# Ten and five wide expert places instead of eleven and five, the last two narrow, and a weight ring cut later, in a two-layer transformer kernel

## The chip, the cores and the metric

The kernel runs on one core of a Trainium2 chip, as one program. The metric is the device time of one execution in microseconds (us); the number compared is the median over several executions. Before the change it is 1600.03 us (three runs, 1596.84 to 1610.28).

## What is computed

The reference is a two-layer transformer trunk on 256 image tokens and 256 context tokens of width 1024. Each layer has a mixer (a gated linear attention, a Fourier mix and a windowed attention, merged by gates) and then a mixture of 16 experts. Layer 0 sends all 512 tokens through its experts, layer 1 only the 256 image tokens; a final norm follows. The change lies in the experts' part:

```python
def hierarchical_moe(h, w_router_group, w_router_expert, w1, w3, w2):
    ...
    expert_id = g_sel[:, None] * MOE_EXPERTS_PER_GROUP + top_idx
    ...
    for e in range(MOE_EXPERTS):
        hid = jax.nn.silu(h @ w1[e]) * (h @ w3[e])
        out = out + (hid @ w2[e]) * gates[:, e:e + 1]
    return out
```

Every token has two experts. An expert's three matrices (1024x512, 1024x512, 512x1024, float32) are 6 MiB.

## The kernel before

The order of the program is mixer 0, experts 0, mixer 1, experts 1, final norm (`body`). The kernel does not run each expert over all tokens. It sorts the tokens by expert and works through 16 **places** in a fixed order (`moe`); which expert stands at which place is decided on the chip. The first `STAT` places (two in layer 0, three in layer 1) hold experts 0, 1 (and 2); the other experts are ranked by their number of tokens, and the ranks are dealt first to the wide places and then to the narrow ones (`place_ranks`).

- A **wide** place, `B` in `PLACES`, has room for 128 tokens. Each weight piece is split by ScalarE and VectorE into a high and a low part (`split`, lines 265 and 266), and TensorE makes three products per pair of tiles (`mm3`, lines 235 to 237): 72 products of 128x512 in a place.
- A **narrow** place, `s`, has room for 64 tokens. The weights are used as they are, in float32, without splitting. `pair` (line 1643) sets two products side by side in the column halves of TensorE: `w1` and `w3`, and later the two column halves of `w2`. The trace shows 32 + 16 records of line 1643 in a place.

If an expert has more tokens than its place has room, a branch (`tc.If`, line 1768) runs `moe_general`, which goes through all 16 experts again for every 256 tokens.

**Weights and ring.** A place's weights come in six pieces of 1 MiB, 96 in a layer, loaded by DMAs that SyncE's queue issues in the order of `pieces_of` (all have line 245 in the profile). In that order stand, for place q, the second halves of its `w1` and `w3`, the first piece or pieces of place q+1 (one for a wide place, two for a narrow one), and the two `w2` pieces of place q; counted from 1, the `w2` pieces of the last places are 84 and 85 or later. Each piece gets the next slot of a ring (`ring`). In layer 0 the ring has 12 slots: six of its own, two of the pool `raw`, and four **spare** ones; in layer 1 it has 13. A piece's DMA is issued when the piece that last held the slot has been used, and SyncE's queue is in order, so nothing behind it is issued earlier. After `CUT` pieces the spare slots drop out as they come up, and eight (nine) are left. The spare slots are wanted at the end of the stage:

- For the places up to the last but two, outputs are scaled by the gate (`ye`, lines 1719 and 1732) and scattered to a table `yb` in HBM by GpSimd's indirect DMA (line 1561).
- The outputs of the last two places stay on the chip: line 1739 and line 1740 write their high and low parts into spare slots (`yes`).
- `rows` (line 1747) loads the scattered outputs back in token order, two rows for each token, into spare slots, after the last weight piece; GpSimd adds the two (line 1748).
- `put_rows` adds the last two places with products against a one-hot matrix (line 1759) and the loaded rows with a product against the identity (line 1762), into one PSUM tile for each 512 columns; part of it stands before the branch of line 1768 and part behind.
- Then the sum is scaled (line 1780), added to `x` (line 1782), and in layer 1 normed and written out (lines 407, 408, 416, 1847, 1848).

The tile framework schedules each engine's order from the program's order and its dependencies; instructions of neighbouring places interleave. TensorE starts the next place's first products before the current place's `w2` products.

The functions that the change touches and what calls them:

Of the kernel before, what the change touches and what calls it, by code (L numbers as in the profile page):

```python
# [8 lines left out]
F32 = mybir.dt.float32  # L9
F32R = mybir.dt.float32r  # L10
# [3 lines left out]
AF = mybir.ActivationFunctionType  # L14
OP = mybir.AluOpType
# [4 lines left out]
P = 128  # L20
# [4 lines left out]
NE = 16  # L25
CAP = (128, 128)
SM = 64

STAT = (2, 3)
PLACES = ("BBsBBsBBsBBsBsBB", "BBBsssssssssssBB")  # L30
RING = (6, 7)
ONCE = (0, 2)
AHEADG = 2
CUT = 50
EXTRA = 2
EA = 8
EB = 1
# [10 lines left out]
def consts():  # L48
# [47 lines left out]
    for l in range(2):  # L96
        big = np.array([x == "B" for x in PLACES[l]])
        pos[:, l, 0] = NE - 1 - np.arange(NE) + 1.0e5 * np.maximum(0, STAT[l] - np.arange(NE))
# [9 lines left out]
def place_ranks(l):  # L108

    n = STAT[l] + PLACES[l][STAT[l]:].count("B")  # L110
    big, small = iter(range(n)), iter(range(n, NE))
    return [next(big if x == "B" else small) for x in PLACES[l]]


def ts(i, n):
    return slice(i * n, (i + 1) * n)
# [12 lines left out]
class Net:  # L129
# [1126 lines left out]
    def ring(self):  # L1256

        self.piece += 1
        if self.piece > CUT:

# [5 lines left out]
    def pieces_of(self, l):  # L1266
# [9 lines left out]
        def up(w, q, c):  # L1276
            return (w, q, c), self.wload(src(w, q)[ts(c, 512), :], 4, 512, self.ring())
# [5 lines left out]
        def begin(q):  # L1283
            for w in ("w1", "w3")[:1 + (PLACES[l][q] == "s")]:
                yield up(w, q, 0)
        self.eid = {}
        yield from begin(0)
        for q in range(NE):
            yield up("w1", q, 1)
            if PLACES[l][q] == "B":  # L1290
                yield up("w3", q, 0)
# [109 lines left out]
    def moe(self, l):  # L1401
        nc, io, tc = self.nc, self.io, self.tc
        T = 2 * SEQ if l == 0 else SEQ
        nt = T // P
        ns, cap = T // SEQ, CAP[l]
        big = [x == "B" for x in PLACES[l]]
        dp, h2b, yb, lg = self.dp, self.h2b, self.yb, self.lg
# [3 lines left out]
        def tl(shape, name, dt=F32):  # L1411
            return dp.tile(shape, dt, name=name)
        V = nc.vector
# [46 lines left out]
        for c in range(2):  # L1460
            pt = self.c1()
            for k in range(4):
                for t in range(nt):
                    nc.tensor.matmul(pt[:, ts(k, cap)], self.h2[:, t, ts(4 * c + k, P)], self.oh0[:, t],
                                     start=(t == 0), stop=(t == nt - 1))
# [45 lines left out]
        yp = self.pool(sr, "moey", bufs=3, side="right")  # L1511
# [3 lines left out]
        gsl = tl([P, NE], "gsl")  # L1515
# [116 lines left out]
        def up(ps, xx, w, e, c):  # L1632

            for u, (wh, wl) in enumerate(self.halves(w, e, c)):
                for k in range(2):
                    kk = 4 * c + 2 * u + k
                    self.mm3(ps, xx[0][:, kk, :], xx[1][:, kk, :], wh[:, k, :], wl[:, k, :], kk == 0, kk == KD - 1)

        def pair(ps, xs, ws, k0, n):

            for k in range(n):
                for i, w in enumerate(ws):
                    nc.tensor.matmul(ps[ts(i, SM)], xs[:, k0[0] + k, :], w[:, k, :], start=(k0[0] + k == 0),  # L1643
                                     stop=(k0[0] + k == k0[1] - 1))

        def begin(e, xx):
            ps = self.pA()
            if big[e]:
                up(ps, xx, "w1", e, 0)
            else:  # L1650
                pair(ps, xx, [self.piece_at(w, e, 0) for w in ("w1", "w3")], (0, KD), 4)
            return ps
# [6 lines left out]
        def hidden(th, n):  # L1659
            pt = self.c3()  # L1660
            for k in range(4):
                nc.tensor.transpose(pt[:, ts(k, n)], th[:, ts(k, P)], self.ident[:n, :n])
            return pt[:, :4 * n]
        yes = []
        p1 = begin(0, xx)
        for e in range(NE):
            if big[e]:
# [6 lines left out]
            if big[e]:  # L1674
# [5 lines left out]
                pt = hidden(th, cap)  # L1680
# [3 lines left out]
            else:  # L1684
# [4 lines left out]
                pt = hidden(th, SM)  # L1689
# [11 lines left out]
            if e == NE - 2:  # L1701
# [4 lines left out]
                oh = rp.tile([P, 2, T], F32R, name="oh")  # L1706
                for i in range(2):
                    for t in range(nt):
                        V.tensor_scalar(oh[:cap, i, ts(t, P)], self.iotab[:cap], float(P * t - 1), tkf[:cap, e + i:e + i + 1],
                                        op0=OP.add, op1=OP.is_equal)  # L1710
                rq = self.pool(sr, "rows2", bufs=2, side="right") if nt > 2 else None
            if not big[e]:
                p2 = self.c2()
                for c in range(2):
                    w = self.piece_at("w2", e, c)
                    for k in range(2):
                        pair(p2, hs, [w[:, k:k + 1, ts(o, 512)] for o in range(2)], (2 * c + k, 4), 1)
                ye = yp.tile([P, 512], F32, name="ye")
                nc.scalar.activation(ye, p2, AF.Copy, scale=gsl[:, e:e + 1])  # L1719
                put = (ye, e)  # L1720
                continue
            p2 = [self.c2(), self.c2()]
            for c in range(2):
# [5 lines left out]
            if e < NE - 2:  # L1729
                ye = yp.tile([P, D], F32, name="ye")  # L1730
                for o in range(2):
                    nc.scalar.activation(ye[:, ts(o, 512)], p2[o], AF.Copy, scale=gsl[:, e:e + 1])
                put = (ye, e)
                continue
            ye = self.spare.pop(0).tile([P, 2048], F32, name="wraw").bitcast(F32R).rearrange("p (h d) -> p h d", h=2)
            yes.append(ye)
            for o in range(2):
                q = ts(o, 512)
                nc.scalar.activation(ye[:cap, 0, q], p2[o][:cap], AF.Copy, scale=gsl[:cap, e:e + 1])
# [1 line left out]
                                       op0=OP.mult, op1=OP.subtract)  # L1741
# [11 lines left out]

        def put_rows(t, pt, js):

            for o in range(2):
                for j in js:
                    for u in range(2):
                        nc.tensor.matmul(pt[o], oh[:cap, j, ts(t, P)], yes[j][:cap, u, ts(o, 512)],  # L1759
                                         start=(j + u == 0), stop=False)  # L1760
                if 1 in js:
                    i = nc.tensor.matmul(pt[o], self.ident, yrs[t][:, 0, ts(o, 512)], start=False, stop=True)  # L1762
                    self.lates += [i] if t >= 2 else []
        pts = [[self.pA(), self.pA()], [self.c1(), self.c1()]]
        for t in range(2):
            put_rows(t, pts[t], (0,))
# [4 lines left out]
        for t in range(nt):  # L1771
            self.pri.append(tc.cur_priority)
            yr = yrs[t]
            if t < 2:
                pt = pts[t]
                put_rows(t, pt, (1,))
            else:
                pt = [self.c1(), self.c2()]
                put_rows(t, pt, (0, 1))
            i = [V.tensor_mul(yr[:, 1, ts(o, 512)], pt[o], gb[:, t // 2, ts(o, 512)]) for o in range(2)]  # L1780
            self.later += i if t >= 2 else []
            V.tensor_add(self.x[:, t], self.x[:, t], yr[:, 1])
# [116 lines left out]
```

## Time and profile before

| | us |
|---|---|
| median of three runs | 1600.03 |
| lowest, highest | 1596.84, 1610.28 |
| the profiled execution, device time | 1606.12 |
| its span, first to last instruction | 1604.30 |
| PE (TensorE) busy | 1465.3 |
| VectorE busy | 972.2 |
| ScalarE busy | 765.4 |

PE is TensorE's products, PEld its weight loads, DVE is VectorE, ACT ScalarE, POOL GpSimd, SP SyncE. Times in the rows count from the span's start. A wait is shown as idle time in front of an instruction, with what ended it. Places are counted from 0 to 15.

### The profile page before, as it was taken

To read this page: it belongs to the slowest core of one execution; us is meant where nothing else is said; L and a number is where in the kernel's file an instruction comes from. 1 tells how busy PE (TensorE), PEld (TensorE's weight loads), DVE (VectorE), ACT (ScalarE), POOL (GpSimd) and SP (SyncE) were. 2 spreads that over 40 slices of the span, in tenths; PEclk is the share of its full clock that TensorE was granted. 3 is DMA by queue.
4 is the path that set the end of the run, shared out by engine and by line. 5 is a ranking of instruction groups with operands and counts; after the bars stand their busy time and mean duration, and the time that the engine had idled before them with its cause. 6 is when DMAs were issued, how large, how long until landed. Compare 5 with 4: busy or idle time off the path is not lost. (4 is left out here: it accounts for less than half of the span.)

```text
span 1604.3 us, 22319 instructions
## 1 busy us (share of the span) xinstructions
PE 1465.3 (91%) x8165; PEld 1038.6 (65%) x8165; DVE 972.2 (61%) x1771; ACT 765.4 (48%) x1306; POOL 237.7 (15%) x244
## 2 busy tenths in 40 slices
PE   6999899999999996899998888999899979998885
PEld 4666666577777796666665466787689967432253
DVE  4468667433377776877674477558865679211166
ACT  4658556422223333566664455657664448211152
POOL 2024100000112103201110014013101121021001
PEclk9999999999999998999999899999999989999998
DMA  9762342543556687699999853422334689999991
GB/s 317 217 199 89 104 134 80 171 124 118 176 178 213 194 276 277 219 361 395 335 375 338 334 193 98 120 80 84 101 123 162 221 322 333 369 380 402 399 382 43
DMA packets 218379, 362.44 MB, mean 226 GB/s; under 512 B 25722, under 2 KB 100676, under 8 KB 218261
## 3 DMA queue, kind: packets, MB, share of 16 engines
q1 hardware_dynamic: 211520, 349.77, 62.7%
q0 software_dynamic: 6304, 11.04, 2.0%
q8 instruction: 68, 1.11, 0.3%
q14 instruction: 51, 0.41, 0.1%
q10 hardware_dynamic: 436, 0.10, 0.0%
HBM read 350.82 MB, written 21.04 MB: 232 GB/s over the span
## 5 line engine op out<-in xcount | busy, mean ns | idle before, releaser
L266 DVE TENSOR_TENSOR wlo<-wraw,whi 128x1024 fp32r<-128x1024 f32 (+1 forms) x334 | 402.5, 1218 | 205.9 <-ACT whi L265 130.3
L265 ACT ACTIVATE whi<-wraw 128x1024 fp32r<-128x1024 f32 (+1 forms) x334 | 332.2, 1011 | 264.0 <-PE pa L229 120.8
L228 PE MATMUL pa<-hhi,whi 128*128 128x512 f32 (+1 forms) x704 | 243.6, 361 | 1.9 <-ACT kT L792 0.9
L229 PE MATMUL pa<-hlo,whi 128*128 128x512 f32 (+1 forms) x704 | 240.3, 356 | 0.7 <-DVE hlo L551 0.7
L228 PEld LDWEIGHTS pa<-hhi,whi 128*128 128x128 f32 x704 | 134.9, 192 | 37.1 <-issue 16.2
L231 PE MATMUL pa<-hhi,wlo 128*128 128x512 f32 (+1 forms) x704 | 151.2, 348 | 0.0
L229 PEld LDWEIGHTS pa<-hlo,whi 128*128 128x128 f32 x704 | 135.1, 192 | 24.2 <-issue 9.6
L1643 PE MATMUL pa<-wraw,xh 128*64 128x512 f32 x464 | 132.7, 613 | 2.9 <-DMA wraw<-in_w_dram 2.5
L231 PEld LDWEIGHTS pa<-hhi,wlo 128*128 128x128 f32 x704 | 113.6, 190 | 20.4 <-issue 6.2
L235 PE MATMUL pa<-whi,xh 128*128 128x512 f32 x224 | 94.6, 422 | 13.4 <-ACT whi L265 12.7
L236 PE MATMUL pa<-wlo,xh 128*128 128x512 f32 x224 | 96.5, 431 | 9.0 <-DVE wlo L266 8.9
L1656 DVE SCALAR_TENSOR_TENSOR th<-th,pa 128x512 f32<-128x512 f32 (+1 forms) x32 | 21.8, 680 | 130.7 <-ACT th L1655 130.7
L763 POOL TENSOR_TENSOR m<-m,gu 128x512 f32<-128x512 f32 (+1 forms) x32 | 40.1, 1254 | 402.1 <-DVE gu L761 402.1
L237 PE MATMUL pa<-whi,xl 128*128 128x512 f32 x224 | 93.1, 416 | 0.0
L1643 PEld LDWEIGHTS pa<-wraw,xh 128*64 128x64 f32 x464 | 37.6, 139 | 67.5 <-issue 59.5
L1555 POOL DMA_INDIRECT xg<-h2b,tki x30 | 34.9, 1164 | 249.6 <-PE c L1618 103.1
L1719 ACT ACTIVATE ye<-c,gsl 128x512 f32<-128x512 f32 x16 | 11.0, 687 | 124.5 <-PE c L1643 124.5
L1643 PE MATMUL c<-wraw,hh 128*64 128x512 f32 x256 | 70.3, 601 | 0.0
L236 PE MATMUL pa<-y,whi 128*128 128x512 f32 (+1 forms) x192 | 66.3, 345 | 0.9 <-DVE y L272 0.9
L235 PEld LDWEIGHTS pa<-whi,xh 128*128 128x128 f32 x224 | 44.8, 200 | 33.1 <-ACT whi L265 18.8
L235 PE MATMUL pa<-y,whi 128*128 128x512 f32 (+1 forms) x192 | 65.5, 341 | 0.7 <-DVE m L757 0.7
L237 PE MATMUL pa<-y,wlo 128*128 128x512 f32 (+1 forms) x192 | 65.1, 339 | 0.0
(459 smaller groups left out, 2894.7 us busy)
## 6 DMA issues: line engine op xcount, KB each, us to landing
wraw<-in_w_dram SPq DMA_DIRECT2D x182, 1024.0 KB
wraw<-in_w_in_dram SPq DMA_DIRECT2D x44, 1024.0 KB
adaw<-in_w_ada_dram SPq DMA_DIRECT2D x80, 512.0 KB
x<-in_w_dram SPq DMA_DIRECT2D x10, 1024.0 KB
adaw<-in_w_ada_dram SPq DMA_DIRECT2D x8, 1024.0 KB
wraw<-in_w_out_dram SPq DMA_DIRECT2D x8, 1024.0 KB
yb<-zero SPq DMA_DIRECT2D x12, 512.0 KB
wraw<-yb SPq DMA_DIRECT2D x6, 1024.0 KB
```

Of the source, the lines that this page charges most:

```text
L228: mm(out, lh, rh, start=(i == 0), stop=False)
L229: mm(out, lh, rl, start=False, stop=False)
L231: self.mm = mm(out, ll, rh, start=False, stop=(i == len(ops) - 1))
L235: mm(out, lh, rh, start=start, stop=False)
L236: mm(out, lh, rl, start=False, stop=False)
L237: self.mm = mm(out, ll, rh, start=False, stop=stop)
L265: self.sp = nc.scalar.activation(hv[:, :, q], v[:, :, q], AF.Copy)
L266: self.sl = self.lo.tensor_sub(lv[:, :, q], v[:, :, q], hv[:, :, q].bitcast(F32))
L763: nc.gpsimd.tensor_add(self.m[:, j, :], self.m[:, j, :], u[:, :TY])
L1555: return nc.gpsimd.indirect_dma_start(out=xgs[e % len(xgs)][:n], out_offset=None, in_=h2b, in_offset=bass.IndirectOffsetOnAxis(ap=tki[:n, ...
L1643: nc.tensor.matmul(ps[ts(i, SM)], xs[:, k0[0] + k, :], w[:, k, :], start=(k0[0] + k == 0), stop=(k0[0] + k == k0[1] - 1))
L1656: V.scalar_tensor_tensor(th, th, 1.0, p1, op0=OP.add, op1=OP.mult)
```

## The change

The table of places is new in both layers, with one wide place fewer in layer 0 (ten), and narrow places at the end: three in layer 0, four in layer 1. `CUT` goes from 50 to 84. For a narrow place among the last two, the output stays in a spare slot as well: high and low part, with the two column halves on the two partition halves, as the narrow products leave them; the one-hot products then contract 64 partitions for each half. In `put_rows` the loops change places, so that the two column halves follow each other.

```diff
-PLACES = ("BBsBBsBBsBBsBsBB", "BBBsssssssssssBB")
+PLACES = ("BBBBsBBsBBsBBsss", "BBBsssBssssBssss")
...
-CUT = 50
+CUT = 84
...
+        def last_y(e):
+
+            ye = self.spare.pop(0).tile([P, 2048], F32, name="wraw").bitcast(F32R).rearrange("p (h d) -> p h d", h=2)
+            yes.append(ye)
+            return ye
...
-                ye = yp.tile([P, 512], F32, name="ye")
-                nc.scalar.activation(ye, p2, AF.Copy, scale=gsl[:, e:e + 1])
-                put = (ye, e)
+                if e < NE - 2:
+                    ye = yp.tile([P, 512], F32, name="ye")
+                    nc.scalar.activation(ye, p2, AF.Copy, scale=gsl[:, e:e + 1])
+                    put = (ye, e)
+                    continue
+
+                ye = last_y(e)[:, :, :512]
+                nc.scalar.activation(ye[:, 0], p2, AF.Copy, scale=gsl[:, e:e + 1])
+                V.scalar_tensor_tensor(ye[:, 1], p2, gsl[:, e:e + 1], ye[:, 0].bitcast(F32), op0=OP.mult, op1=OP.subtract)
                 continue
...
-            ye = self.spare.pop(0).tile([P, 2048], F32, name="wraw").bitcast(F32R).rearrange("p (h d) -> p h d", h=2)
-            yes.append(ye)
+            ye = last_y(e)
...
+            for j in js:
+                for u in range(2):
+                    for o in range(2):
+                        if big[NE - 2 + j]:
+                            lh, rh = oh[:cap, j, ts(t, P)], yes[j][:cap, u, ts(o, 512)]
+                        else:
+                            lh, rh = oh[ts(o, SM), j, ts(t, P)], yes[j][ts(o, SM), u, :512]
+                        nc.tensor.matmul(pt[o], lh, rh, start=(j + u == 0), stop=False)
             for o in range(2):
-                for j in js:
-                    for u in range(2):
-                        nc.tensor.matmul(pt[o], oh[:cap, j, ts(t, P)], yes[j][:cap, u, ts(o, 512)],
-                                         start=(j + u == 0), stop=False)
                 if 1 in js:
```

Behind the diff, lines of the kernel after stand 11 to 15 higher: 1759 becomes 1774, 1762 becomes 1777, 1748 becomes 1759, 1768 becomes 1783; the narrow eviction of the last places is line 1731.

How the order moves, at three places. ScalarE at the end of layer 1, before: places 14 and 15 are wide (`whi` the splits, `hh` the hidden values, `wraw<-c` the outputs kept in spare slots).

```order
L271 ACTIVATE hh<-c_14420 128x512
L265 ACTIVATE whi<-wraw 128x1024 x6
L1739 ACTIVATE wraw<-c_14477,gsl 128x512
L1739 ACTIVATE wraw<-c_14478,gsl 128x512
L265 ACTIVATE whi<-wraw 128x1024 x2
L1655 ACTIVATE th<-pa 128x512
L265 ACTIVATE whi<-wraw 128x1024 x4
L265 ACTIVATE whi<-x 128x1024
L271 ACTIVATE hh<-c_14599 128x512
L265 ACTIVATE whi<-x 128x1024
```

The same end after: places 12 to 15 are narrow (`th` the gating, `xh` a place's tokens, `ye` an output that is scattered).

```order
L1726 ACTIVATE ye<-c_14331,gsl 128x512
L1693 ACTIVATE th<-pa 64x512
L1655 ACTIVATE th<-pa 64x512
L1620 ACTIVATE xh<-c_14433 128x512
L1726 ACTIVATE ye<-c_14407,gsl 128x512
L1693 ACTIVATE th<-pa 64x512
L1655 ACTIVATE th<-pa 64x512
L1731 ACTIVATE wraw<-c_14495,gsl 128x512
L1693 ACTIVATE th<-pa 64x512
L1655 ACTIVATE th<-pa 64x512
L1731 ACTIVATE wraw<-c_14536,gsl 128x512
```

The splits are gone from the last places, and each is left with two gating steps and one kept output.

TensorE from the last place's `w2` products to the branch in layer 1, before (`c` and `pa` are PSUM tiles, `oh` the one-hot matrix).

```order
L235 MATMUL c_14609<-whi,hh 128x512
L236 MATMUL c_14609<-wlo,hh 128x512
L237 MATMUL c_14609<-whi,hl__14605 128x512
L1759 MATMUL pa<-wraw,oh 128x512
L1759 MATMUL c_14667<-wraw,oh 128x512
L1759 MATMUL pa<-wraw,oh 128x512 x2
L1762 MATMUL pa<-wraw,ident 128x512
L1767 TENSOR_LOAD cnti
L1768 COMPARE_AND_BRANCH
```

The same after, from the last place's first products on.

```order
L1643 MATMUL pa<-wraw,xh 64x512 x7
L1774 MATMUL pa<-wraw,oh 128x512 x2
L1662 MATMUL c_14529<-ident,th 128x64 x4
L1643 MATMUL c_14536<-wraw,hh 64x512 x8
L1774 MATMUL pa<-wraw,oh 128x512 x2
L1774 MATMUL c_14561<-wraw,oh 128x512
L1774 MATMUL c_14562<-wraw,oh 128x512
L1782 TENSOR_LOAD cnti
L1783 COMPARE_AND_BRANCH
```

The last place's `w2` products are 8 narrow instructions (of four passes, in 16 records) where 24 wide ones stood, and no identity product stands ahead of the branch any more.

GpSimd at the end of layer 1, before (line 1748 adds the loaded rows, line 1803 is the body of the branch not taken, line 408 the norm).

```order
L1561 DMA yb_8905<-ye,yki 1024x512 x6
L1748 TENSOR_TENSOR wraw<-wraw 128x1024 x2
L1767 TENSOR_LOAD cnti
L1768 COMPARE_AND_BRANCH
L1803 COMPARE_AND_BRANCH
L1803 UNCONDITIONAL_BRANCH x2
L1895 BRANCH_PREFETCH_HINT
```

The same after.

```order
L1759 TENSOR_TENSOR wraw<-wraw 128x1024
L1782 TENSOR_LOAD cnti
L1783 COMPARE_AND_BRANCH
L1818 COMPARE_AND_BRANCH
L1818 UNCONDITIONAL_BRANCH x2
L1910 BRANCH_PREFETCH_HINT
L1818 REGISTER_ALU
L1818 COMPARE_AND_BRANCH
L1818 UNCONDITIONAL_BRANCH
L1783 UNCONDITIONAL_BRANCH
L1759 TENSOR_TENSOR wraw<-wraw 128x1024
L408 TENSOR_TENSOR rsr<-rsr,nhalf 128x1 x2
```

The second of the two adds has moved behind the branch.

## Rows read from the trace of the kernel before

**Rows 1.** The page, span in 40 slices (40.1 us each): TensorE's clock, DMA share.

```profile
PEclk9999999999999998999999899999999989999998
DMA  9762342543556687699999853422334689999991
```

**Rows 2.** Windows in layer 0's experts: length, PE, PEld, DVE, ACT, POOL busy, clock, DMA, GB/s.

```profile
674.17:795.81 121.64, 121.64 (x592) 80.09 (x591) 92.16 (x136) 77.90 (x93) 15.53 (x13) 1.00 1.00 371
795.81:958.66 162.85, 146.74 (x585) 92.01 (x584) 98.83 (x105) 83.86 (x101) 18.50 (x13) 0.92 0.83 306
...
788.00:800.00 12.00, 12.00 (x67) 6.42 (x63) 4.45 (x6) 3.65 (x5) 0.00 (x0) 1.00 0.78 270
...
900.00:905.00 5.00, 4.62 (x12) 2.41 (x11) 3.48 (x5) 1.10 (x3) 0.00 (x0) 0.50 1.03 396
```

**Rows 3.** Timeline of ScalarE: outputs of places 0-2, 4, 5, 7, 10-13 and 15.

```profile
674.17 1.25 ACT L1732 ACTIVATE ye<-c,gsl 128x512 f32<-128x512 f32 x2
...
694.01 1.24 ACT L1732 ACTIVATE ye<-c,gsl 128x512 f32<-128x512 f32 x2
...
706.62 0.69 ACT L1719 ACTIVATE ye<-c,gsl 128x512 f32<-128x512 f32 x1 [2.53 <-PE c L1643]
...
744.31 1.25 ACT L1732 ACTIVATE ye<-c,gsl 128x512 f32<-128x512 f32 x2
...
758.58 0.69 ACT L1719 ACTIVATE ye<-c,gsl 128x512 f32<-128x512 f32 x1 [2.54 <-PE c L1643]
...
795.81 1.39 ACT L1732 ACTIVATE ye<-c,gsl 128x512 f32<-128x512 f32 x2 [2.45 <-PE c L237]
...
851.86 1.26 ACT L1732 ACTIVATE ye<-c,gsl 128x512 f32<-128x512 f32 x2 [2.69 <-PE c L237]
868.61 0.69 ACT L1719 ACTIVATE ye<-c,gsl 128x512 f32<-128x512 f32 x1 [9.10 <-PE c L1643]
892.97 1.26 ACT L1732 ACTIVATE ye<-c,gsl 128x512 f32<-128x512 f32 x2 [2.69 <-PE c L237]
911.12 0.69 ACT L1719 ACTIVATE ye<-c,gsl 128x512 f32<-128x512 f32 x1 [10.02 <-PE c L1643]
958.66 1.39 ACT L1739 ACTIVATE wraw<-c,gsl 128x512 fp32r<-128x512 f32 x2 [2.44 <-PE c L237]
```

**Rows 4.** Timeline of SyncE's queue from 777.9 to 790.0 us.

```profile
777.47 11.02 SPq L245 DMA_DIRECT2D wraw<-in_w_dram  x2
```

**Rows 5.** Timeline of TensorE: narrow `w2` products in layer 0.

```profile
702.92 3.65 PE L1643 MATMUL c<-wraw,hh 128*64 128x512 f32 x16
```

**Rows 6.** VectorE's costliest group from 690 to 796 us.

```profile
L266 DVE TENSOR_TENSOR wlo<-wraw,whi 128x1024 fp32r<-128x1024 f32 x49 | 59.4, 1225 | 20.8 <-ACT whi L265 20.5
```

**Rows 7.** Windows in layer 1's experts, columns as in rows 2.

```profile
1340.00:1560.00 220.00, 195.24 (x929) 91.51 (x928) 73.84 (x119) 69.21 (x94) 26.61 (x25) 0.97 1.03 388
...
1564.00:1566.00 2.00, 1.33 (x6) 0.75 (x4) 2.00 (x1) 1.74 (x3) 1.92 (x1) 1.00 0.12 47
1566.00:1584.00 18.00, 14.08 (x57) 9.80 (x57) 13.62 (x12) 7.13 (x8) 3.20 (x1) 1.00 0.00 1
```

**Rows 8.** Timelines at the end of the span: SyncE, GpSimd, ScalarE, VectorE, TensorE.

```profile
1548.42 2.46 SPq L1747 DMA_DIRECT2D wraw<-yb  x2
...
1563.52 5.71 POOL L1748 TENSOR_TENSOR wraw<-wraw 128x1024 f32<-128x1024 f32 x2 [21.23 <-SPq L1768]
...
1582.76 1.38 ACT L1739 ACTIVATE wraw<-c,gsl 128x512 fp32r<-128x512 f32 x2 [2.37 <-PE c L237]
...
1583.48 1.45 DVE L1740 SCALAR_TENSOR_TENSOR wraw<-c,gsl,wraw 128x512 fp32r<-128x512 f32 x2 [1.84 <-ACT wraw L1739]
...
1588.70 0.47 PE L1759 MATMUL pa<-wraw,oh 128*128 128x512 f32 x1 [2.90 <-PEq L1768]
```

**Rows 9.** The chain that ended last, one step: start, us, what.

```profile
1593.26 0.87 PE c L1762 x2
```

## The prediction

> **What bounds the kernel now.** I read the page's slices first [rows 1]: TensorE's clock is high nearly throughout, and DMA is full in two stretches, the experts of layer 0 (about 680 to 960) and of layer 1 (1340 to 1584). There I read windows, ScalarE's outputs as marks of where each place ends, then the queues and the end of the span.
>
> Layer 0, places 1 to 7 (five wide, two narrow): TensorE is busy 121.64 of 121.64 us at clock 1.00, which is 2.4 GHz, and DMA is at 1.00 with 371 GB/s [rows 2]. Both are full; TensorE sets the pace. Places 8 to 15 (again five wide, but three narrow): TensorE is busy 146.74 of 162.85 us, at clock 0.92, with DMA down to 0.83 [rows 2]. So the same kind of work loses time in the second half.
>
> Pace of a place [rows 3]: the narrow ones took 706.62 − 694.01 = 12.61 and 758.58 − 744.31 = 14.27, mean 13.44 us; a wide one is (121.64 − 2 × 13.44) / 5 = 18.95 us. At that pace places 8 to 15 are 5 × 18.95 + 3 × 13.44 = 135.1 us. They took 162.85, so 27.8 us are lost: 16.1 of them as TensorE's idle time, the other 11.7 as products at lower clock. The marks show where: narrow places 11 and 13 ended 16.75 and 18.15 us after the place ahead, not 13.44, and ScalarE waited 9.10 and 10.02 us for them [rows 3].
>
> The cause I read from SyncE. It issues two pieces at 777.47, then nothing for 11.02 us [rows 4], and DMA falls to 0.78 in 788 to 800 [rows 2], while TensorE is still full. Those are the pieces just behind number 50: four of the twelve slots drop out, and a piece now waits for the one eight places earlier in the ring instead of twelve. TensorE uses up the lead and waits from then on. The queue is in order, so everything behind stands too.
>
> **Layer 0, part by part.** *The table.* Places 1 to 7 hold five wide and two narrow ones again: nothing. Places 8 to 15 become four wide and four narrow: one wide turns narrow, 18.95 − 13.44 = 5.5 us less.
>
> *The cut at 84.* Pieces 51 to 84 keep twelve slots, so the gap of 11.02 us goes, and the 27.8 us can go with it. What is late next? First, the DMA. At 777.47 some 56 pieces are issued, 40 are left; 1.0486 MB at 371 GB/s is 2.83 us, together 113 us, so the last lands at 890 to 900. The last `w2` piece is wanted some 4 us [rows 5] before place 15's output, at 795.81 + 129.6 − 4 = 921. The lead holds if DMA averages above 41.9 MB / 143.5 us = 292 GB/s; it kept 306 even with the stalls [rows 2]. Second, the drop-out itself, moved to the end: the last four pieces wait for slots used eight pieces earlier. Between that use and their own stand three bursts of narrow products, 16 records of 3.65 us each [rows 5], 11.0 us; two pieces need 5.7 us to move. The trace of before doesn't show this; bounds are 0 and the whole of the old gap, 11.0 [rows 4]. I take 3, nearer to the row of 3.65 us bursts. Third, VectorE in the four wide places in a row at the start: 12 splits of 1225 ns [rows 6] are 14.7 us, and some 3.4 us of gating beside them make 18.1 of 18.95. It stays covered, barely; if the cover goes, 1 to 2 us.
>
> The kept outputs of narrow places 14 and 15 replace wide ones: one column-half pair of ScalarE and VectorE instructions instead of two. In `put_rows` the loops only change places. For layer 0's hand-over bounds are −1 and +2 us; I take 0.
>
> Sum for layer 0: 5.5 + 27.8 − 3 = **30 us** (range 20 to 33).
>
> At the lower clock: in 900 to 905 the granted clock was 0.50, which is 1.2 GHz, with DMA at 1.03, right behind waits [rows 2]. The Trainium skill (TensorE: Matmul & The Clock Gate, section "HAM oscillation — how this bites in real kernels") says that a TensorE which waits for DMA between groups falls back and starts each group slow, so that one wait is paid twice. The trace agrees: 16.1 us of idle come with 11.7 us of slow products. By that rule any wait left in the late narrow places would cost about 1.7 times itself; the sum above does not use it.
>
> **Layer 1.** Here DMA is the bound: 1.03 and 388 GB/s over 220 us, with TensorE at 195.24 [rows 7]. A place's pieces take 6 × 1.0486 / 0.388 = 16.2 us; a wide place wants 18.95, a narrow one 13.44. Five wide and eleven narrow stay, so weights land when they did. What changes is what is left behind the last piece. Before, places 14 and 15 are wide: DMA is at 0.12 in 1564 to 1566 and 0.00 in 1566 to 1584, while TensorE works 14.08 of those 18 us [rows 7], until the last output at 1582.76 [rows 8]. After, four narrow places end the layer; each is 2.8 us faster than its pieces, so the two wide places among the others (2.7 us slower each) are made up, and TensorE follows the DMA.
>
> The new end: all landed by about 1565, of which the row loads, issued last [rows 8], are 2 MB or 5 us; the last weight lands at about 1560. Last `w2` piece, 8 records: half of 3.65 [rows 5], 1.8, to 1562. One kept output: half of 1.38, then half of 1.45 [rows 8], to 1563.4. Four one-hot products of at most 0.47 [rows 8]: 1565. The branch: 2.90 [rows 8]: 1568. From there to the last pair before it took 1593.26 − 1588.70 = 4.6 us [rows 8, 9]: 1572.6.
>
> GpSimd runs beside this. It adds the rows at 1563.52, 5.71 us for two [rows 8]. After, the second add stands behind the branch: first add to 1566.4, branch 2.9 to 1569.3, second to 1572.2. It is just in time for the last pair, so it costs nothing there; with GpSimd's branch longer by x, it costs x. From the last pair at 1593.26 [rows 9] to the span's end at 1604.30 are 11.0 us, unchanged: 1583.6. Gain **21 us** (18 to 24).
>
> **Sum.** 30 + 21 = 51 us. The profiled execution is 1606.1 (span 1604.3 and 1.8 around it), 6.1 above the median and inside the spread of the runs. 1606.1 − 51 = 1555; on the median, 1600.0 − 51 = **1549 us**, its own range 1538 to 1560. A measurement of this kernel tells about 1% from no change.
>
> **Rivals.**
> *The late narrow places of layer 0 wait still (18%).* Three narrow places in a row eat pieces each 2.24 us (13.44 / 6), DMA brings one each 2.83, and only the lead of up to twelve pieces pays for it. For: places 11 and 13 show just this [rows 3]. Against: 20 us between the landing and the need above. If half of the 27.8 returns, +14: 1563; if all, 1577. In three places at 1.2 GHz throughout it would be up to 3 × 13.4 = 40 us.
> *Layer 1's end is set by the rows (8%).* GpSimd waited 21.23 us before its adds, put down to SyncE's queue [rows 8], so when the rows really came in is known only from DMA's end. If scatter, load or the add behind the branch come 10 us late, 1559.
> *The change does not do what it says (4%).* TensorE's loss in the second half of layer 0 comes from something else than slots, and in layer 1 the weights land later by what the end saves: 5.5 us from the table alone, 1594.
> *Slower (3%).* With one wide place fewer an expert of over 64 tokens may stand at a narrow place: then the branch is taken and all 16 experts run again, for layer 0 twice: 2 × 96 × 1.0486 MB at 388 GB/s [rows 7] is 519 us, 2070 in all. It decides from the 65th token. By the reference's routing of its inputs, layer 0's ninth expert by rank has 56 tokens and layer 1's third has 42, so both tables hold; only a tie or a rounding of the router far from what is seen could break it. The same mechanism in layer 1 is 259 us.
>
> **How the numbers follow.** My case 67%, at 1549. The range for 8 in 10 goes down to 1536 (both gains at their upper end, 33 + 24 = 57 us, and the clock of 0.97 in layer 1 [rows 7] full, 3% of 220 us or 6.6) and up to 1577, which holds the first two rivals and leaves out the last two and the slow clock. Faster by over 1% (below 1584): my case and the first two rivals, 0.93; within 1%, the third, 0.04; slower 0.03.
>
> **What would show it.** In the profile after: layer 0's last kept output near 925 to 930 instead of 958.66; TensorE busy and clock 1.00 and DMA near 1.0 from 795 to 900; SyncE's long gap among the last pieces only. Layer 1: last kept output at 1562 to 1564, less what layer 0 gave, and some 20 us from it to the span's end. Wrong, if TensorE waits or its clock falls in the last three places of layer 0, if DMA in layer 1 is clearly below 1.0, or if the last pair waits for GpSimd.

## The result and the profile after

Seven runs of the kernel after have a median of 1584.03 us (1578.78 to 1591.61); seven of the kernel before have 1604.22. The ratio is 0.9892 (95% interval 0.9861 to 0.9922): 1.1% faster, where I had forecast 3.2% and a range that ended at 1577. The sign was right, the size was not.

The page after, TensorE's clock and DMA in 40 slices of 39.6 us, which answers to [rows 1]:

```profile
PEclk9999999999999997999999988999999989999998
DMA  9762242443556578699999763322336689999992
```

Windows after, columns as in [rows 2]: layer 0's places 1 to 7, places 8 to 15, of these the last three; layer 1 from the first place's output to the last's, of this its last four places, and its last 16 us.

```profile
670.49:792.55 122.06, 122.04 (x605) 83.06 (x604) 98.80 (x143) 83.80 (x99) 14.86 (x13) 1.00 1.02 377
792.55:939.75 147.20, 134.02 (x558) 74.89 (x558) 71.57 (x82) 65.16 (x81) 16.67 (x13) 0.94 0.93 339
892.03:939.75 47.72, 39.34 (x150) 12.44 (x148) 6.11 (x10) 6.67 (x11) 6.67 (x4) 0.86 0.80 299
...
1318.55:1563.19 244.64, 220.32 (x1013) 106.73 (x1011) 89.73 (x135) 82.65 (x112) 31.44 (x27) 0.96 0.96 356
1501.00:1563.19 62.19, 50.99 (x202) 16.38 (x200) 7.90 (x13) 9.03 (x16) 7.65 (x5) 0.89 0.73 280
...
1547.00:1563.19 16.19, 13.49 (x44) 4.08 (x42) 2.26 (x4) 1.19 (x3) 4.70 (x2) 0.79 0.02 8
```

Places 1 to 7 took 122.06 us (121.64 before), places 8 to 15 took 147.20 (162.85): 15.7 us gained, of 30 forecast. TensorE is still idle for 13.2 us there, and in the last three places its clock is 0.86. Layer 1 took 244.64 us; before, from 1338.45 to 1582.76, it took 244.31. So the four narrow places at its end brought nothing, although in its last 16 us nothing is loaded any more. The rest is small: 3.7 us ahead of the first output of layer 0, 1.0 us between the layers, and 2.7 us at the end (18.8 us from the last kept output to the span's end, 21.5 before). Together 15.7 − 0.4 − 0.3 + 3.7 + 1.0 + 2.7 = 22.4, which but for rounding is the spans' difference (1604.3 to 1582.0).

The outputs of layer 0's places 13 to 15 and layer 1's places 14 and 15 on ScalarE (line 1726 is an output that is scattered, line 1731 a kept one):

```profile
908.05 0.69 ACT L1726 ACTIVATE ye<-c,gsl 128x512 f32<-128x512 f32 x1 [10.27 <-PE c L1643]
...
924.83 0.69 ACT L1731 ACTIVATE wraw<-c,gsl 128x512 fp32r<-128x512 f32 x1 [12.09 <-PE c L1643]
...
939.75 0.69 ACT L1731 ACTIVATE wraw<-c,gsl 128x512 fp32r<-128x512 f32 x1 [7.79 <-PE c L1643]
...
1546.01 0.69 ACT L1731 ACTIVATE wraw<-c,gsl 128x512 fp32r<-128x512 f32 x1 [10.76 <-PE c L1643]
...
1563.19 0.69 ACT L1731 ACTIVATE wraw<-c,gsl 128x512 fp32r<-128x512 f32 x1 [9.20 <-PE c L1643]
```

The last narrow places take 16.8 and 14.9 us in layer 0, 17.2 in layer 1, not the 13.44 of my sum. SyncE's long gap has moved, as forecast, but it is longer than I took: the queue stands 15.1 us ahead of piece 93 in layer 0, inside the row of six pieces that spans 22.90 us, and DMA falls to 0.37 in 900 to 910. The row, SyncE's longest wait in 880 to 912 (us in total, times, longest), and the window:

```profile
888.95 22.90 SPq L245 DMA_DIRECT2D wraw<-in_w_dram  x6
```

```profile
SPq L245 <- PE c L1643: 16.2, 2, 15.1
```

```profile
900.00:910.00 10.00, 10.00 (x41) 3.13 (x38) 0.00 (x0) 0.69 (x1) 0.98 (x1) 0.83 0.37 131
```

Is it this gap that ate the gain? TensorE's waits say no. In the timeline of TensorE from 892 on (the second column is modelled) it waits for `th`, the gating, and in no row for a weight:

```profile
892.39 4.50 PE L1643 MATMUL pa<-wraw,xh 128*64 128x512 f32 x18
898.88 0.43 PE L1662 MATMUL c<-ident,th 64*128 64x64 f32 x4 [1.98 <-DVE th L1657]
899.24 4.92 PE L1643 MATMUL pa<-wraw,xh 128*64 128x512 f32 x13
...
907.43 4.03 PE L1643 MATMUL pa<-wraw,xh 128*64 128x512 f32 x17
914.32 0.66 PE L1662 MATMUL c<-ident,th 64*128 64x64 f32 x4 [2.86 <-DVE th L1657]
914.91 6.03 PE L1643 MATMUL pa<-wraw,xh 128*64 128x512 f32 x13
```

After the second wait 13 records take 6.03 us, where 17 took 4.03 before it.

### The profile page after: what moved, and what is told of

Same layout as the page of the kernel before. It is cut to its first block, busy times and chain, and to the rows that moved or that the text cites. A ratio compares the mean times of both kernels' runs of the same rounds, so it can differ in the third digit from the quotient of the medians.

```text
span 1582.0 us, 22237 instructions
## 1 busy us (share of the span) xinstructions
PE 1452.4 (92%) x8141; PEld 1020.5 (65%) x8141; DVE 942.1 (60%) x1753; ACT 752.1 (48%) x1292; POOL 232.5 (15%) x244
## 5 line engine op out<-in xcount | busy, mean ns | idle before, releaser
L266 DVE TENSOR_TENSOR wlo<-wraw,whi 128x1024 fp32r<-128x1024 f32 (+1 forms) x324 | 377.2, 1177 | 186.3 <-ACT whi L265 121.5
L265 ACT ACTIVATE whi<-wraw 128x1024 fp32r<-128x1024 f32 (+1 forms) x324 | 321.7, 1009 | 239.4 <-PE pa L229 114.6
L1643 PE MATMUL pa<-wraw,xh 128*64 128x512 f32 x520 | 151.4, 636 | 0.0
L1656 DVE SCALAR_TENSOR_TENSOR th<-th,pa 64x512 f32<-64x512 f32 (+1 forms) x32 | 21.7, 679 | 124.2 <-ACT th L1655 124.2
L1643 PEld LDWEIGHTS pa<-wraw,xh 128*64 128x64 f32 x520 | 42.8, 144 | 76.5 <-issue 74.5
L235 PE MATMUL pa<-whi,xh 128*128 128x512 f32 x208 | 85.0, 408 | 7.4 <-ACT whi L265 6.9
L236 PE MATMUL pa<-wlo,xh 128*128 128x512 f32 x208 | 85.8, 413 | 2.9 <-DVE wlo L266 2.8
L237 PE MATMUL pa<-whi,xl 128*128 128x512 f32 x208 | 83.4, 401 | 0.0
L349 DVE SCALAR_TENSOR_TENSOR adaw<-adaw,cT 128x512 f32<-128x512 f32 x56 | 49.1, 877 | 15.8 <-DMA adaw<-in_w_ada_dram 15.2
L1561 POOL DMA_INDIRECT yb<-ye,yki x28 | 28.5, 1018 | 198.5 <-ACT ye L1726 109.1
```

What stands on the lines that cost most here:

```text
L235: mm(out, lh, rh, start=start, stop=False)
L236: mm(out, lh, rl, start=False, stop=False)
L237: self.mm = mm(out, ll, rh, start=False, stop=stop)
L265: self.sp = nc.scalar.activation(hv[:, :, q], v[:, :, q], AF.Copy)
L266: self.sl = self.lo.tensor_sub(lv[:, :, q], v[:, :, q], hv[:, :, q].bitcast(F32))
L349: nc.vector.scalar_tensor_tensor(v[:, j], v[:, j], ck, acc, op0=OP.mult, op1=OP.add)
```

## The experiments

Two theories stood against each other. **A**: TensorE's order against ScalarE and VectorE decides; it waits for splits and for the gating, and runs slowly afterwards. **B**: SyncE's stalls, so slots and weights, decide. All runs are compared with the kernel before on the same chip. Columns in us, read as in [rows 3] from ScalarE's outputs of the profiled execution; "tail" is from the last output to the span's end. In e11 and e12 places 8 to 15 hold two wide and six narrow ones, so this column compares only with itself there.

| run | median | ratio to before (95%) | L0 places 8–15 | of these 13–15 | layer 1 | of this 12–15 | tail |
|---|---|---|---|---|---|---|---|
| before | 1604.2 | 1 | 162.9 | 65.7 | 244.3 | 76.5 | 21.5 |
| after | 1584.0 | 0.9892 (0.9861–0.9922) | 147.2 | 47.7 | 244.6 | 62.2 | 18.8 |
| e1 ring alone | 1602.4 | 1.0012 (0.9993–1.0031) | 155.4 | 59.3 | 243.7 | 75.4 | 21.4 |
| e2 tables alone | 1588.3 | 0.9899 (0.9866–0.9932) | 148.4 | 47.8 | 245.7 | 62.2 | 20.6 |
| e3 up first | 1569.3 | 0.9785 (0.9754–0.9816) | 140.6 | 40.2 | 235.2 | 51.8 | 20.4 |
| e4 L1 wide first | 1576.5 | 0.9830 (0.9802–0.9859) | 148.1 | 47.6 | 233.4 | 55.6 | 22.4 |
| e5 order alone | 1585.7 | 0.9889 (0.9857–0.9922) | 145.0 | 48.1 | 244.1 | 76.8 | 21.5 |
| e6 fill | 1580.1 | 0.9865 (0.9833–0.9897) | 138.0 | 40.7 | 239.8 | 57.9 | 22.8 |
| e7 e3 and e4 | 1570.4 | 0.9799 (0.9766–0.9831) | 139.7 | 40.1 | 235.2 | 64.2 | 20.6 |
| e8 L0's table alone | 1585.5 | 0.9898 (0.9868–0.9929) | 145.7 | 46.1 | 243.5 | 77.5 | 19.1 |
| e9 e3, cut 50 | 1572.4 | 0.9837 (0.9806–0.9867) | 140.0 | 40.5 | 236.3 | 52.7 | 20.5 |
| e10 e3, fill last | 1564.4 | 0.9785 (0.9750–0.9820) | 133.8 | 35.8 | 230.0 | 46.7 | 22.4 |
| e11 e3, L0 wide first | 1560.0 | 0.9754 (0.9723–0.9785) | 119.0 | 41.9 | 234.8 | 52.9 | 21.2 |
| e12 all | 1556.1 | 0.9711 (0.9680–0.9741) | 119.9 | 42.9 | 231.8 | 48.5 | 21.7 |

**The cut by itself.** The kernel before with

```diff
-CUT = 50
+CUT = 84
```

> The kernel before with the cut at 84 instead of 50, tables as they were. Theory A (the late cut does free layer 0, and what was lost again in the kernel after is lost in its own late narrow places): places 8 to 15 of layer 0, 162.85 us before, come to 140 to 147; layer 1 (244.3 us from the first place's output to the last's) stays within 3; total 15 to 22 us less. Rival B (the late cut is worth little because SyncE only stalls later, 15.08 us at the end of layer 0 and 10.51 us in layer 1 in the kernel after): places 8 to 15 come to 155 or more, layer 1 gets 5 to 10 us longer; total within 10 us of before.

Measured: nothing, 1.0012. In places 8 to 15 the DMA runs on through 788 to 800, yet TensorE waits for the same things as long as before. Its chief waits in places 8 to 15, before and in this run (us in total, times, longest):

```profile
PE pa L235 <- ACT whi L265: 8.7, 6, 2.3
PE pa L236 <- DVE wlo L266: 3.8, 4, 1.9
PE c L236 <- DVE wlo L266: 1.6, 2, 1.1
```

```profile
PE pa L235 <- ACT whi L265: 8.7, 6, 2.3
PE pa L236 <- DVE wlo L266: 4.0, 4, 1.9
PE c L236 <- DVE wlo L266: 1.7, 2, 1.1
```

More pieces on the chip don't shorten a wait for a split. The 7 us that places 8 to 15 show less are at a clock of 0.98 instead of 0.92 [rows 2] in this one execution; the median shows none of it.

```profile
796.40:951.70 155.30, 138.81 (x585) 86.10 (x584) 98.36 (x105) 83.78 (x101) 18.08 (x13) 0.98 0.86 321
```

So the waits of these places are the same in both executions, and what the slow products behind them cost is not: up to 7.5 of the 15.7 us that this stretch gained from before to after may be the clock of before's one profiled execution. Theory A's number for this run was wrong as well: it still gave the cut 15 to 22 us.

**The tables by themselves.** The kernel after with `CUT = 50`.

> The kernel after with the cut at 50 again. Theory A: layer 0's places 8 to 15 go back to 155 to 160 us (147.2 after), layer 1 (244.6 after) stays within 3, since its end is set by TensorE in the last narrow places; total 8 to 13 us more than after. Rival B: layer 1 loses its 10.51 us stall of SyncE and gets 8 to 10 us shorter, layer 0 gets 5 to 8 longer; total within 3 us of after.

Measured: 0.9899 against 0.9892 of after. Layer 1 keeps its 245.7 us without the stall, so Rival B falls there; layer 0 stays at 148.4, so Theory A falls on layer 0, which I had still put down to the ring. The tables carry the change; the cut carries nothing that can be told.

**The order by itself.** Then what was lost in places 8 to 15 of before? On ScalarE, where narrow place 11 hands over to wide place 12, the kernel before shows this:

```profile
855.94 0.59 ACT L1687 ACTIVATE th<-pa 64x512 f32<-64x512 f32 x1 [2.82 <-PE pa L1643]
856.55 0.59 ACT L1655 ACTIVATE th<-pa 64x512 f32<-64x512 f32 x1
857.04 2.00 ACT L265 ACTIVATE whi<-wraw 128x1024 fp32r<-128x1024 f32 x2
858.93 0.58 ACT L1620 ACTIVATE xh<-c 128x512 f32<-128x512 f32 x1
```

The wide place's first splits (L265) stand in ScalarE's queue behind the narrow place's gating (L1687, L1655), which waits for TensorE; then the output of place 11, 9.10 us of waiting [rows 3], stands ahead of the next splits. TensorE stands idle in front of the products that need them:

```profile
858.14 0.50 PE L235 MATMUL pa<-whi,xh 128*128 128x512 f32 x1 [2.27 <-ACT whi L265]
...
870.29 0.50 PE L235 MATMUL pa<-whi,xh 128*128 128x512 f32 x1 [1.35 <-ACT whi L265]
871.55 0.49 PE L236 MATMUL pa<-wlo,xh 128*128 128x512 f32 x1 [0.76 <-DVE wlo L266]
```

If that is it, the same places in another order lose nothing, with the cut at 50 and its stall. The code after, with

```diff
-PLACES = ("BBBBsBBsBBsBBsss", "BBBsssBssssBssss")
+PLACES = ("BBsBBsBBBBBBBsss", "BBBsssssssssssBB")
-CUT = 84
+CUT = 50
```

> The code after with cut 50, layer 1's table of before and, in layer 0, before's eleven wide and five narrow places in another order: places 8 to 15 hold five wide, then three narrow, as many as before. Theory C (what places 8 to 15 lose in the kernel before is lost where a wide place follows a narrow one: its first splits stand in ScalarE's queue behind the narrow place's gating and kept output): the waits of L235 and L236 for splits, 14.3 us before, fall below 4, places 8 to 15 take 140 to 148 us instead of 162.85, total 12 to 20 us less than before. Rival B (the ring's cut at 50, as I predicted): places 8 to 15 stay at 155 or more, total within 8 us of before.

Measured: 0.9889, the whole gain of the change, with eleven wide places and the old cut. Places 8 to 15 take 145.0 us, and 0.5 us is left of the waits for splits; what TensorE waits for now is the gating:

```profile
PE c L1662 <- DVE th L1657: 6.1, 3, 2.9
PE pa L1774 <- DVE th L1656: 2.1, 1, 2.1
...
PE pa L235 <- ACT whi L265: 0.5, 1, 0.5
```

The stall at the cut is still there (the queue stands 13.1 us, as SyncE's waits in 777.9 to 800 show, and DMA is at 0.74) and TensorE does not feel it:

```profile
SPq L245 <- DVE wlo L266: 20.6, 4, 13.1
```

```profile
788.00:800.00 12.00, 12.00 (x69) 9.60 (x68) 10.32 (x12) 9.11 (x11) 0.00 (x0) 1.00 0.74 272
```

Theory C of this run is confirmed in its numbers, with the total at 18.8 us, and in the main in its mechanism. Two things limit it. Of the 14.1 us of waits for splits that before has in places 8 to 15, 10.2 stand in the wide places right behind narrow ones and 3.5 in the last two, 14 and 15; the new order moves both away. And not every such hand-over loses. At those from places 2, 5 and 8 of before TensorE waits 0, 0 and 0.6 us for splits, at those from 11 and 13 it waits 4.4 and 5.1. At the first three, ScalarE's order has a split of the wide place ahead of the narrow place's gating; at the other two it has none. Place 2 of before:

```profile
695.14 1.05 ACT L265 ACTIVATE whi<-wraw 128x1024 fp32r<-128x1024 f32 x1
698.06 0.59 ACT L1687 ACTIVATE th<-pa 64x512 f32<-64x512 f32 x1 [1.86 <-PE pa L1643]
```

So it is the order on the queue that costs, not the neighbourhood alone. Why the schedule differs from place to place is open.

**Layer 0's table by itself.** The kernel after with layer 1's table of before.

> The kernel after with layer 1's table of before; layer 0 as after. Theory D (layer 1's new table gave nothing, the whole gain is layer 0's): layer 1 takes 242 to 246 us from the first place's output to the last's, total within 4 us of after (1584). Rival (layer 1's table gave its part, hidden by something else in that layer): layer 1 takes 250 or more, total 1592 to 1600.

Measured: 1585.5 against 1584.0, layer 1 at 243.5. Layer 1's table gave nothing.

**The gating's wait.** Where a narrow place follows a narrow one, TensorE gets the next place's first 16 products before the transposes that need the gating:

```diff
+                early = e + 1 < NE and not big[e + 1]
+                if early:
+                    pn = begin(e + 1, xn)
...
-                pt = hidden(th, SM)
+                pt = hidden(th, SM, self.lp if early else None)
...
+                if first is not None:
+                    self.behind(i, first)
```

(`self.lp` is the last of these products; `behind` sets the order on TensorE.)

> The kernel after; where a narrow place follows a narrow one, TensorE does the next place's first 16 products before the transposes that wait for the gating. Theory A (in the late narrow places TensorE waits 2.0 to 2.9 us for the gating and runs the next 7 us at 1.2 GHz): layer 0's places 13 to 15, 47.7 us after, come to 38 to 42, layer 1's places 12 to 15, 62.2 us, to 52 to 56; total 12 to 18 us less than after. Rival B (SyncE's stalls and so the weights set the pace there): both within 3 us of after, TensorE waits for the weights instead.

Measured: 14.7 us less than after, as Theory A had it. Layer 0's last three places took 12.1, 11.4 and 16.6 us, layer 1's last four 51.8, with layer 0's last piece issued at 908.6 us instead of 911.5 (SyncE stood 11.2 us there). TensorE waited for no weight in these places, so the weights were there all along.

**Useless work in the same wait.** 24 transposes, whose result nothing reads, between the narrow place's products and the transposes that wait; the wait itself stays.

```diff
+        def fill(e):
+            pd, i = self.c1(), self.lp
+            for k in range(24):
+                j = nc.tensor.transpose(pd[:, ts(k % KD, SM)], xgs[e % len(xgs)][:SM, ts(k % KD, P)], self.ident[:SM, :SM])
+                self.behind(j, i)
+                i = j
+            return i
...
-                pt = hidden(th, SM)
+                pt = hidden(th, SM, fill(e) if e >= 12 else None)
```

> The kernel after with 24 useless transposes of TensorE in each of the places 12 to 15 that is narrow, between its w1 and w3 products and the transposes that wait for the gating; nothing else moves. Theory A1 (half of what the late narrow places lose is the fall to 1.2 GHz after the wait, so that filling the wait with useless work pays): granted clock in layer 0's places 13 to 15 rises from 0.86 to 0.95 or more, they take 40 to 44 us instead of 47.7, layer 1's places 12 to 15 take 54 to 58 instead of 62.2; total 8 to 14 us less than after. Rival A2 (only the wait itself counts): clock or not, both stay within 2 us; total within 3 us of after or more.

Windows of the last three places of layer 0 and the last four of layer 1:

```profile
892.48:933.20 40.72, 38.52 (x230) 16.19 (x229) 7.61 (x18) 6.79 (x11) 1.96 (x2) 1.00 0.63 228
1495.90:1553.80 57.90, 54.06 (x314) 22.58 (x313) 11.29 (x17) 9.28 (x16) 7.72 (x5) 0.97 0.79 303
```

The clock went from 0.86 to 1.00 and from 0.89 to 0.97, and the places took 40.7 and 57.9 us, within what A1 expected. The total did not follow: 4 us less in the medians, half of the lower bound, and the ratios' intervals overlap. In the profiled execution the tail grew by 4.0 us (after's 18.8 is the shortest in the table) and the stretches ahead of the two layers, which the edit does not touch, by 4.7; whether that is always so was not tried. That these waits are paid for a second time in slow products is shown in the places; what it is worth in the total stays open between nothing and these 4 us.

**Layer 1, wide places first.** `"BBBBBsssssssssss"` instead of `"BBBsssBssssBssss"`.

> The kernel after with layer 1's table as five wide places and then eleven narrow ones. Theory A (the wide place at 11 puts TensorE behind the weights, and four narrow places at 15.6 us against 16.2 of DMA can't make it up): the last kept output comes 8 us or less behind the last weight's landing instead of some 20; layer 1 takes 230 to 235 us, total 9 to 14 us less than after. Rival B (weights land later when the wide places are all at the start, since the ring is full sooner and SyncE stands): layer 1 stays within 3 us of 244.6.

Measured: 7.6 us less than after, a little under Theory A's 9 to 14; layer 1 at 233.4 is inside. The loads now end at about 1550, 4 us ahead of the last kept output at 1553.6. Of the 11.3 us that layer 1 gained, places 1 to 11 give 4.6; only these can come from the late wide places. The other 6.6 are in the last four places, which are narrow in both kernels, with TensorE's products in the same order and no shorter waits here. Place 13 of layer 1, first here and then in after, and the window of the last four here:

```profile
1518.07 0.43 PE L1662 MATMUL c<-ident,th 64*128 64x64 f32 x4 [2.86 <-DVE th L1657]
1518.43 3.22 PE L1643 MATMUL pa<-wraw,xh 128*64 128x512 f32 x13
```

```profile
1521.59 0.66 PE L1662 MATMUL c<-ident,th 64*128 64x64 f32 x4 [2.87 <-DVE th L1657]
1522.18 4.48 PE L1643 MATMUL pa<-wraw,xh 128*64 128x512 f32 x13
```

```profile
1498.05:1553.63 55.58, 43.46 (x198) 14.36 (x194) 7.90 (x13) 8.45 (x14) 6.38 (x5) 1.00 0.94 365
```

The clock stays at 1.00 here, where after has 0.89, and each of the four places takes 13.7 to 14.3 us with its wait in it. So a wait of 2.9 us does not always bring slow products. What decides it is not shown. The lower clock is not the luck of one execution: after and e2 both have 0.89 in these places, and in layer 0's last three after, e2, e4 and e5 all have 0.86. The full clock of e4 is seen in one.

Both edits together:

> The kernel after with both edits: the next narrow place's first products ahead of the transposes, and layer 1's wide places all at the start. If both act on TensorE's lag behind the weights at the end of layer 1, they don't add fully, since the last weight's landing becomes the bound: layer 1 takes 226 to 232 us (235.2 and 233.4 with one of them), total 1559 to 1566. If they act on different things, layer 1 takes 224 or less, total 1558 or less. If the weights land later with the wide places first, layer 1 takes 233 or more, total 1567 or more.

Measured: 1570.4, no better than `up_first` alone (1569.3); layer 1 is 235.2 in both. The first case fell by its own number. The last one fits by its numbers but not by its reason, as the weights do not land later: the loads end about 230 us after the layer's first output, and in after about 229. TensorE now waits for weights, more than in any run above, where it is at most 3.3 us (its waits in 1400 to 1564):

```profile
PE pa L1643 <- DMA wraw<-in_w_dram: 5.8, 4, 1.9
```

The loads end 228 to 230 us after the first output in after, e3, e4, e7 and e10 alike. The 235.2 us here are still some 5 behind that; e10 below, at 230.0, is almost at it.

**Is the cut worth something once TensorE is free?** `up_first` with `CUT = 50`.

> The run up_first (1569.3, from which TensorE no longer waits for the gating in the late narrow places) with the cut at 50 again. Theory E (the cut decides nothing in either form, because TensorE waits for splits and gating and not for slots): layer 0 from place 0 to 15 and layer 1 stay within 3 us of 262.7 and 235.2, total within 4 us of 1569. Rival (the cut was only hidden by TensorE's own waits, and with these gone it shows): places 8 to 15 of layer 0 get 5 to 12 us longer than 140.6, total 1574 or more. A third way: SyncE's stall of 11.15 us at the end is the worse one, and with the cut at 50 the total falls below 1564.

Measured: 1572.4, ratio 0.9837 against 0.9785, the intervals overlap; layer 0 the same to 1 us. Theory E holds within 4 us; a gain of some us by the later cut is not excluded.

**The last place, and layer 0's order.** `up_first` with `fill` in the last place alone, then with `"BBBBBBBBBBssssss"` in layer 0.

> The run up_first with 24 useless transposes in the last place alone, where nothing is left that could stand in the wait for the gating. In up_first the last place takes 16.6 us in layer 0 and 16.9 in layer 1 against 11.4 for the one ahead, with 2.65 us of wait and its w2 products at 1.2 GHz. Theory A1 (the clock is half of it): 12.5 to 14.5 us in both layers, total 4 to 8 us less than 1569. Rival A2 (clock high, but the useless work delays the products behind it, or the tail behind the last place takes it back): total within 3 us of 1569.

> The run up_first with layer 0's ten wide places first and its six narrow ones last. Theory C goes on (every narrow place with a wide one behind it costs): two such places are left in places 8 to 15 and one in 1 to 7 of up_first; places 0 to 15 of layer 0 fall from 262.7 us to 250 to 257. Rival D1 (the weights are now the bound in layer 0 as they are in layer 1: 96 pieces at 2.83 us or more from the start of the stage): places 0 to 15 take 260 to 266 and TensorE waits for DMA in the narrow places; total within 4 us of 1569. Rival D2 (VectorE's splits can't keep up over ten wide places): wide places at 20.5 us or more, 268 or more.

Measured: the last place took 12.3 us in layer 0 and 11.7 in layer 1, a little less than A1 asked for, and the total fell by 5.0 (1564.4). Its ratio to before stayed at 0.9785, though, as the kernel before was faster on that chip too, so the total's gain is not shown. With all wide places first, places 0 to 15 took 248.7 us against 262.7, below what Theory C asked for, and 1560.0 in all; its ratio's interval still overlaps that of e3. TensorE is busy for 239.7 of them and DMA full, so both are now near their ends:

```profile
670.60:919.30 248.70, 239.72 (x1162) 157.47 (x1160) 168.67 (x226) 149.31 (x181) 35.09 (x26) 0.99 1.02 377
```

All of it in one kernel:

> The run up_first_l0_wide_first (1560.0) with the useless transposes of the last place too. If the last place's wait and its slow products are on the path in both layers, as in e10 (which gained 5 us on up_first), the total is 1553 to 1557. If layer 0 is bound by the weights by now (its places 14 and 15 took 14.6 and 15.8 us with waits for DMA), only layer 1 gains and the total is 1556 to 1560.

Measured: 1556.1, ratio 0.9711: 2.9% faster than before and 1.8% faster than the change itself. The useless work gained in layer 1 (231.8 against 234.8) and not in layer 0, whose last places wait for weights; 1556.1 lies at the seam of the two cases.

## Why the prediction was wrong, step by step

**What bounds the kernel, layer 0.** The pace of places 1 to 7 was right, and so was the loss of 27.8 us in places 8 to 15. The step that failed is "The cause I read from SyncE". A gap of the queue and a fall of DMA stood just ahead of TensorE's waits, and I took the one for the cause of the other. TensorE's own waits named the splits: in places 8 to 15 of before, TensorE and ScalarE have no wait for a weight, and VectorE has 0.4 us of them. I used ScalarE's wait of 9.10 us [rows 3] as a mark of late places only; it was the mechanism, a queue in which the next splits stand behind an instruction that waits for TensorE. Run e1 takes the cause away that I named and leaves the waits; e5 keeps it and has 0.5 us of waits for splits.

Two readings on the way were wrong too. The marks [rows 3] do not show the loss in the narrow places alone: by my own prices places 11 and 13 lost 8.0 us, but wide place 12 took 24.4 us and lost 5.4, and wide places 14 and 15 took 47.5 together and lost 9.6. And the row of 11.02 us [rows 4] holds both issues, the first at its start and the second at its end; the longest of SyncE's waits there is 9.3 us:

```profile
SPq L245 <- DVE wlo L266: 15.2, 2, 9.3
```

The 11.7 us of slow products are no fixed part of that loss either: e1 has 16.5 us of idle time in the same places, as much as before, with 3.8 us of slow products.

**"One wide turns narrow, 5.5 us less."** Not seen. With eleven wide places e5 does places 8 to 15 in 145.0 us, after with ten in 147.2: after still has one narrow place with a wide one behind it among them, and 4.7 us of waits for splits.

**"I take 3" for the late drop-out.** SyncE stood 15.1 us, more than my upper bound of 11.0. It cost nothing that the runs can tell, since TensorE waited for none of these pieces.

**13.44 us for a narrow place, in both layers.** The price was nearly right for a narrow place at full clock, even among narrow neighbours: 13.7 to 14.3 us in layer 1 of e4, with the waits for the gating in them. What the sum put at nothing is the slow products behind these waits, though the prediction had priced them at "about 1.7 times" the wait. In the kernel after the narrow places at the end took 14.9 to 16.8 us in layer 0 and 14.3 to 17.2 in layer 1, at clocks of 0.86 and 0.89. That cost layer 0 some 7 us (47.7 − 3 × 13.44). With useful work in the wait (e3) a narrow place takes as little as 11.4 us.

**"TensorE follows the DMA" in layer 1.** This step lost nearly the whole 21 us: layer 1 got 0.3 us longer, and only the 2.7 us of the tail came. The last four places took 62.2 us, the pieces for four take 64.8: 2.6 us are made up and not 11. The wide places at 6 and 11 took 21.4 and 22.5 us, not 18.95, so there was more to make up. So TensorE's last kept output came 16 us behind the end of the loads, where my sum had it 2 us ahead; before it was 18 behind. Run e4 shows both parts: wide places first give 4.6 us, the last four places at full clock 6.6. Two small steps held: the adds on GpSimd were no bound (both from 1547.26 on, long before they were wanted), and the tail kept its length to 3 us.

**The rivals.** "The late narrow places still wait" had the right place and nearly the right size for layer 0 (14 of the 27.8 back; measured 15.7 gained of 30), by the wrong mechanism: not for pieces but for the gating. "The change does not do what it says" had the right reason for layer 0, something else than slots, but gave it no gain beyond the 5.5 us of the table. None of the rivals said that layer 1 would gain nothing while layer 0 gained. On the lower clock the Trainium skill's rule (TensorE: Matmul & The Clock Gate, section "HAM oscillation — how this bites in real kernels") is borne out in part. In e6 the places got faster with the wait filled, at a clock of 1.00 instead of 0.86; the waits that the rule tells of are for DMA, those here were for VectorE. In e4 the same waits came with a clock of 1.00 and no slow products, so they are not always paid twice.

## What to carry to other kernels

A stall of a queue that stands ahead of an engine's waits in time is a suspect only; the wait's own releaser, followed back on its engine to the instruction that stands in front of it, says what is late. The price of a unit of work holds for the clock and the neighbours with which it was measured: ask of every moved unit what stands in its waits, and at what clock it runs behind them. Before a cut or a table is costed, move the order alone: one line of a table, with the suspected stall kept, settled here what the two runs of the ring could not.

## What the runs showed of the hardware

Work that nobody needs made places faster. The last place's narrow `w2` products in layer 1, after:

```profile
1556.74 6.40 PE L1643 MATMUL c<-wraw,hh 128*64 128x512 f32 x16 [0.52 <-DVE hh L1697]
```

and with the useless transposes ahead of them (e6), in layer 0 and in layer 1:

```profile
929.51 3.65 PE L1643 MATMUL c<-wraw,hh 128*64 128x512 f32 x16 [0.52 <-DVE hh L1707]
...
1549.04 4.69 PE L1643 MATMUL c<-wraw,hh 128*64 128x512 f32 x16
```

The same 16 records went from 6.40 us to 4.69 in layer 1; in layer 0 they ran at the full rate of [rows 5]. But useless work is not the only way there: in e4, with no such work and 2.1 us of waiting for the gating in the same place, they ran at the full rate as well.

```profile
1549.93 3.65 PE L1643 MATMUL c<-wraw,hh 128*64 128x512 f32 x16 [0.52 <-DVE hh L1697]
```

What keeps the clock up in e4 and not in after is open.

And the ring was deeper than needed: 13.1 and 15.1 us without a single new piece, in e5 and after, left TensorE without one wait for a weight in layer 0's places 8 to 15.
